# Constant products in the pauses of the opening, an earlier first shift block and another load order, in a one-core transformer block

## The chip, the cores and the metric

The kernel runs on one core of a Trainium2 chip. The time is that of one execution on the device in microseconds (us); lower is better. Three runs of the kernel before were timed, and one more execution was taken with the hardware profiler.

## The reference, cut to what matters

One layer of a diffusion backbone works on 256 latent tokens (x) and 256 context tokens (ctx), each with 1024 channels: a half-step feed-forward block, two token mixers side by side, a second half-step feed-forward block, a last norm. Everything is fp32. This change touches only the beginning:

```python
mod_x = (jax.nn.silu(c) @ w_ada[l] + b_ada[l])[:, None, :]
mod_c = (jax.nn.silu(c_ctx) @ w_ada[l] + b_ada[l])[None, None, :]
sh1x, sc1x, g1x, sh2x, sc2x, g2x, sh3x, sc3x, g3x = jnp.split(mod_x, N_MOD, axis=-1)
...
x = x + 0.5 * g1x * swiglu(modulate(rmsnorm(x, norm_ffn1[l]), sh1x, sc1x), w13_ffn1[l], w2_ffn1[l])
ctx = ctx + 0.5 * g1c * swiglu(modulate(rmsnorm(ctx, norm_ffn1[l]), sh1c, sc1c), w13_ffn1[l], w2_ffn1[l])
```

Here `modulate(h, shift, scale)` is `h * (1 + scale) + shift`, `rmsnorm` divides by the root of the mean square over the channels, and `swiglu` is `(silu(a) * b) @ w2` with `a, b = split(h @ w13)`. So before the first large product can start, two vectors (c and c_ctx) go through silu, are multiplied with blocks of w_ada, and the tokens are normed, scaled and shifted.

## The kernel before

Tokens lie as columns: 512 of them, 256 context and 256 latent, by eight blocks k of 128 channels (KT = 8). Every large product is made in fp32r as three products of split operands (`mm3`, lines 86 to 90): each operand is written as a high part (cast on ScalarE, ACT) and a low part (the difference, on VectorE, DVE), and lines 88 to 90 add low times high, high times low and high times high on TensorE (PE).

The *opening* (lines 97 to 408) has an order written out by hand for PE, ACT, DVE and SyncE (SP, which issues all loads). Behind it a planner, which simulates a timeline (line 30), orders the instructions of each engine. Loads that stand behind the opening in the program can be drawn by it to the front of SP's queue: the second load of the unit matrix (line 574) is issued as the second of all.

The opening goes like this.

1. SP loads the unit matrix, the two vectors c (`cr`, line 112), four tiles of x (`xs`, line 147, 512 KB each), and then for k = 0 and 1 (`first_loads`, line 150) the scale block of w_ada (`ada[KT + k]`), its shift block (`ada[k]`) and six column blocks of w13 (`w`, 384 KB). The table of small vectors (`sm`) comes between k = 0 and k = 1.
2. ACT takes silu of `cr` (162); PE turns it over (169, `ct`) and spreads each vector over all partitions (179, `cb`). A table load for the root follows on ACT (166).
3. ACT and DVE square the x blocks by turns (`sq`, 240 and 242), and PE sums them over the channels with a matrix `ones` of value 1/1024 (250, `st`): for each k four narrow products, eight instructions in fp32.
4. ACT takes the root (226), DVE the reciprocal (228), PE spreads the result over all partitions (262, `rs`: four fp32 products), ACT copies it (266, `rstd1`).
5. For each k: the *scale* column is a product and sum on DVE, one instruction per stream (191, `ada`), then the factor (200, `amul`) and the scaled tokens (364, `xr`). The *shift* column is made on PE: eight transposes of the shift block (277, `ada_turn`), two copies on ACT (280, `at`), sixteen narrow products (288, `ada_rows`), a copy (293, `row`), a small product (299) and the sum on DVE (300, `mod`, `ada_cols`). ACT adds the shift and writes the high part h1h (371), DVE the low part h1l (374). The weights of the block are split on ACT (351, `wh`) and DVE (352, `wl`).
6. PE adds the products of block k into six accumulators (`first_products`), two at a time; between them stand the steps of block k + 1 (lines 391 to 406).

On each engine the instructions of the opening run in this written order: what stands behind a waiting one waits too.

## Time and profile before

| what | us |
|---|---|
| median of three runs | 1014.06 |
| lowest, highest | 1011.98, 1014.34 |
| the profiled execution | 1015.47 |
| its span | 1013.7 |

The profiled execution lies 1.41 us above the median of the runs; its span is the time from its first to its last recorded work, and 1.77 us lie around it. All times in the trace count from the span's start. In lines of the timeline and of the views of waits stand the start, the duration, the engine, the line of the kernel, the operation, "out<-in", the shapes and how often (x4: four instructions drawn together); in brackets the idle time of that engine just before it and what ended it. PEld is the loading of a product's fixed operand, SPq the issue of a load by SP. A fp32 product of 128 columns appears as two instructions. In the chain of waits each line has the start, the duration and the work on the path that ended last. A line of the view by windows has the stretch, its length, the busy time (and instructions) of PE, PEld, DVE, ACT and POOL (GpSimd), the granted clock of PE, the busy share of the DMA engines and the GB/s that they moved.

### The profile page before, as it was taken

Reading aid. Unit: us, or ns where it says so; the run is one execution under the profiler, and the core shown is the slowest. Engines: PE = TensorE matmul, PEld = TensorE weight load, DVE = VectorE, ACT = ScalarE, POOL = GpSimd, SP = SyncE. Lnnn points to the kernel's source line nnn. Section 1 sums busy time; section 2 is a strip of 40 time slices with the busy share of each in tenths; the row PEclk is TensorE's granted clock in tenths of the full one; section 3 lists DMA queues with packets and bytes.
Section 4 is the critical chain, followed back from the end, with each engine's and each line's share of the span. In section 5 each row is a group of like instructions: output and inputs, shape, how many; then the busy total and the mean of one; then the engine's idle time right before and its main releaser. Section 6 shows DMA issues by size and latency. Waiting matters only on the chain.

```text
span 1013.7 us, 16779 instructions
## 1 busy us (share of the span) xinstructions
PE 984.4 (97%) x6792; PEld 907.9 (90%) x6792; DVE 663.9 (65%) x1084; ACT 469.4 (46%) x725; POOL 62.4 (6%) x39
## 2 busy tenths in 40 slices
PE   6999999999999998999999998999999989999996
PEld 4778888888888888999999997999999989999995
DVE  7879999998334335866575538865555766676543
ACT  4454322125222423756575456754444545555541
POOL 0000000000000013000000026000000300000011
PEclk9999999999999999999999999999999999999999
DMA  8647766994322233223133434456566446656651
GB/s 337 231 176 249 235 199 212 349 402 160 104 83 75 84 112 115 64 84 125 43 126 108 158 100 150 125 185 183 181 200 187 153 161 186 185 172 182 185 174 42
DMA packets 49238, 166.84 MB, mean 165 GB/s; under 512 B 5380, under 2 KB 7044, under 8 KB 49160
## 3 DMA queue, kind: packets, MB, share of 16 engines
q1 hardware_dynamic: 49160, 165.77, 50.8%
q8 instruction: 53, 0.87, 0.3%
q14 instruction: 25, 0.20, 0.1%
HBM read 164.70 MB, written 1.05 MB: 164 GB/s over the span
## 4 chain that ended last, share of the span: by engine, by line
PE 91%; DVE 4%; ACT 2%; DMA 1%; issue 1%; POOL 0%; DVEq 0%; SPq 0%; ACTq 0%; POOLq 0%
PE y L88 4%; PE y L89 4%; PE y L90 4%; PE pa L89 3%; PE pb L89 3%; PE pa L88 3%; PE pb L88 3%; PE pb L90 3%; PE pa L90 3%; PE ro L89 2%; PE ro L90 2%; PE ro L88 2%; PE fa L89 2%; PE z L90 2%; PE z L89 2%; PE z L88 2%
## 5 line engine op out<-in xcount | busy, mean ns | idle before, releaser
L79 DVE TENSOR_TENSOR wl<-wr,wh 128x1024 fp32r<-128x1024 f32 (+1 forms) x214 | 248.8, 1164 | 202.0 <-ACT wh L78 201.2
L78 ACT CAST wh<-wr 128x1024 fp32r<-128x1024 f32 (+1 forms) x226 | 227.0, 1006 | 273.2 <-PE y L90 79.2
L191 DVE CUSTOM_DVE_ANT_0 junk<-ada,cb,sm 128x1024 bf16<-128x1024 f32 x96 | 122.9, 1280 | 5.9 <-DMA ada<-in_ada 4.4
L89 PE MATMUL y<-gl,wh 128*128 128x512 f32 (+1 forms) x198 | 72.5, 366 | 0.0
L88 PE MATMUL y<-gh,wl 128*128 128x512 f32 (+1 forms) x198 | 72.4, 366 | 0.0
L90 PE MATMUL y<-gh,wh 128*128 128x512 f32 (+1 forms) x198 | 72.3, 365 | 0.0
L455 POOL TENSOR_TENSOR ssum<-ssum,sq 128x256 f32<-128x256 f32 (+1 forms) x18 | 24.6, 1367 | 727.3 <-ACT sq L454 714.2
L89 PE MATMUL pa<-h1l,wh 128*128 128x512 f32 x152 | 59.1, 389 | 0.0
L88 PE MATMUL pa<-h1h,wl 128*128 128x512 f32 x152 | 59.1, 389 | 0.0
L90 PE MATMUL pa<-h1h,wh 128*128 128x512 f32 x152 | 59.1, 389 | 0.0
L88 PE MATMUL pb<-h1h,wl 128*128 128x512 f32 x152 | 59.1, 389 | 0.0
L89 PE MATMUL pb<-h1l,wh 128*128 128x512 f32 x152 | 59.1, 389 | 0.0
L90 PE MATMUL pb<-h1h,wh 128*128 128x512 f32 x152 | 59.1, 389 | 0.0
L89 PE MATMUL fa<-hxl,wh 128*128 128x258 f32 x176 | 50.8, 289 | 0.0
L88 PE MATMUL fa<-hxh,wl 128*128 128x258 f32 x176 | 50.8, 289 | 0.0
L90 PE MATMUL fa<-hxh,wh 128*128 128x258 f32 x176 | 50.6, 287 | 0.0
L89 PE MATMUL fb<-hxl,wh 128*128 128x258 f32 x176 | 50.1, 284 | 0.0
L89 PE MATMUL z<-g2l,wh 128*128 128x256 f32 x176 | 50.0, 284 | 0.0
L88 PE MATMUL fb<-hxh,wl 128*128 128x258 f32 x176 | 50.0, 284 | 0.0
L90 PE MATMUL fb<-hxh,wh 128*128 128x258 f32 x176 | 49.9, 283 | 0.0
L88 PE MATMUL z<-g2h,wl 128*128 128x256 f32 x176 | 49.8, 283 | 0.0
L90 PE MATMUL z<-g2h,wh 128*128 128x256 f32 x176 | 49.8, 283 | 0.0
(310 smaller groups left out, 2908.3 us busy)
## 6 DMA issues: line engine op xcount, KB each, us to landing
ada<-in_ada SPq DMA_DIRECT2D x72, 512.0 KB, 5.1
wr<-in_w13b SPq DMA_DIRECT2D x44, 512.0 KB, 4.3
wr<-in_w13a SPq DMA_DIRECT2D x38, 512.0 KB, 4.3
wrv<-in_wv SPq DMA_DIRECT2D x16, 512.0 KB, 4.3
wr<-in_wg SPq DMA_DIRECT2D x16, 512.0 KB, 4.2
wr<-in_wgate SPq DMA_DIRECT2D x16, 512.0 KB, 4.3
wr<-in_pret SPq DMA_DIRECT2D x16, 512.0 KB, 3.8
wr<-in_w2b SPq DMA_DIRECT2D x16, 512.0 KB, 3.6
```

Source lines behind the costliest of these rows:

```text
L78: S.copy(hi[:, :n], raw[:, :n])
L79: (lo_engine or V).tensor_tensor(lo[:, :n], raw[:, :n], f32(hi[:, :n]), op=ALU.subtract)
L88: PE.matmul(o, w[1], a[0], start=start, stop=False)
L89: PE.matmul(o, w[0], a[1], start=False, stop=False)
L90: PE.matmul(o, w[0], a[0], start=False, stop=stop)
L191: V.tensor_tensor_reduce(junk, raw, cb[:, s, :], 1.0, sm[:, BIAS + n : BIAS + n + 1], ALU.mult, ALU.add, mod[:, s, n : n + 1],)
L455: G.tensor_tensor(ssum[0][:, cols], ssum[0][:, cols], sq[:, :w], op=ALU.add)
```

## The change

Five things, all in the opening but the last:

- *Order of loads.* The first x tile is loaded ahead of the vectors c. The table `sm` follows the x tiles directly. For each k the shift block is loaded ahead of the scale block.
- *Constant products* (`keep_warm`): `ones` times `ones`, 128 by 128 by 128 in fp32, into the bank that `ct` had or that `rs` will have; nobody reads the results. Six stand ahead of the transposes of `cr`, eleven among the sums of squares (1, 3, 4 and 3 ahead of those of k = 0, 2, 4 and 6), three behind them.
- *The first shift block* is transposed on PE (and copied on ACT) ahead of the spread of the reciprocal, instead of behind it, and its rows are made ahead of the first scale block's steps in the written order.
- *The split of the first weights* is cut in two: 256 columns ahead of h1h and h1l of block 0, 512 behind them, with the same work in all.
- *Two loads* (`dist` and the second `unit`), which the program has far behind the opening, are kept in the program's order.

```diff
+    xs = []
+
+    def load_x(q):
+        t = per.tile([P, 2, 512], F32, name=f"xs{q}")
+        nc.sync.dma_start(t, i["xs"][:, 2 * q : 2 * q + 2, :])
+        xs.extend([t[:, 0, :], t[:, 1, :]])
+
     unit_raw = stp.tile([P, P], F32, name="unit_raw")
     nc.sync.dma_start(unit_raw, i["unit"])
+    load_x(0)
     cr = wtile("wr", "cr")[:, :512]
...
-    for q in range(4):
-        t = per.tile([P, 2, 512], F32, name=f"xs{q}")
-        nc.sync.dma_start(t, i["xs"][:, 2 * q : 2 * q + 2, :])
-        xs += [t[:, 0, :], t[:, 1, :]]
+    for q in range(1, 4):
+        load_x(q)
+    nc.sync.dma_start(sm, i["smalls"])
 
     def first_loads(k):
-        for n in (KT + k, k):
+        for n in (k, KT + k):
...
     first_loads(0)
-    nc.sync.dma_start(sm, i["smalls"])
     first_loads(1)
...
     ps = bank("ct")
+
+    def keep_warm(o, n):
+
+        for _ in range(n):
+            PE.matmul(o, ones, ones, start=True, stop=True, skip_group_check=True)
+
+    idle = ps
+    keep_warm(idle[:, :P], 6)
     for c in range(4):
         PE.transpose(ps[:, c * P : (c + 1) * P], cr[:, c * P : (c + 1) * P], unit_raw)
...
+        keep_warm(idle[:, :P], (1, 0, 3, 0, 4, 0, 3, 0)[k])
         for q in range(4):
             PE.matmul(
                 ps_st[32 * q : 32 * q + 32, :P], ones[:, :32], sq[:, q * P : (q + 1) * P],
...
     r1 = rstd_of(ps_st[:, :P], P, "1q")
     ps_st = bank("rs1")
+    keep_warm(ps_st[:, :P], 3)
+    ada_turn(0)
     rstd1 = stp.tile([P, 512], F32, name="rstd1")
     for q in range(4):
         PE.matmul(
             ps_st[:, q * P : (q + 1) * P], pick[:, q * P : (q + 1) * P], r1, start=True, stop=True
         )
...
-    def first_split(k):
-        hi, lo = wtile("wh", f"wh0_{k}"), wtile("wl", f"wl0_{k}")
-        S.copy(hi[:, :n1], first_w[k][:, :n1])
-        V.tensor_tensor(lo[:, :n1], first_w[k][:, :n1], f32(hi[:, :n1]), op=ALU.subtract)
-        first_hl[k] = hi, lo
+    def first_split(k, c0=0, c1=n1):
+        if k not in first_hl:
+            first_hl[k] = wtile("wh", f"wh0_{k}"), wtile("wl", f"wl0_{k}")
+        c = slice(c0, c1)
+        split(first_hl[k][0][:, c], first_hl[k][1][:, c], first_w[k][:, c])
...
-    ada_turn(0)
+    ada_rows(0)
     first_scaled(0)
-    first_split(0)
-    ada_rows(0)
     ada_cols(0)
+    first_split(0, 0, T)
     first_shifted(0)
+    first_split(0, T, n1)
...
-    nc.sync.dma_start(dist, i["dist"])
+    tc.keep_in_program_order(nc.sync.dma_start(dist, i["dist"]))
...
-    nc.sync.dma_start(raw, i["unit"])
+    tc.keep_in_program_order(nc.sync.dma_start(raw, i["unit"]))
```

## The prediction, as put on record before the result

> **What bounds the kernel now.** I read the page first, then the chain of waits over the first 70 us, then the timeline of the same stretch engine by engine, and last the places where TensorE's clock changes.

> ```profile
> span 1013.7 us, 16779 instructions
> ...
> PE 984.4 (97%) x6792; PEld 907.9 (90%) x6792; DVE 663.9 (65%) x1084; ACT 469.4 (46%) x725; POOL 62.4 (6%) x39
> ```

> TensorE (PE) is busy for 97%, so what the change can win lies in the other 29 us and in the stretches where PE is busy but slow. The opening has most of both. Times and waits of its first part:

> ```profile
> 1.18 0.42 SPq L574 DMA_DIRECT2D unit<-in_unit  x1
> 1.65 0.67 SPq L112 DMA_DIRECT2D cr<-in_cc  x1
> 2.36 1.82 SPq L147 DMA_DIRECT2D xs<-in_xs  x4
> 3.75 0.63 ACT L162 ACTIVATE cr<-cr 128x512 f32<-128x512 f32 x1 [1.52 <-DMA cr<-in_cc]
> 4.39 1.28 ACT L166 ACT_TABLE_LOAD   x1
> 4.43 1.11 PE L169 MATMUL ct<-unit_raw,cr 128*128 128x128 f32 x4 [4.43 <-ACT cr L162]
> 5.69 0.29 ACT L166 ACTIVATE warm<-cr,eps 128x1 f32<-128x1 f32 x1
> 5.97 0.73 SPq L157 DMA_DIRECT2D sm<-in_smalls  x1
> 6.07 0.63 PE L179 MATMUL cb<-crl,one_r 1*128 1x512 f32 x4
> 6.11 0.63 ACT L242 ACTIVATE sq<-xs 128x512 f32<-128x512 f32 x1
> 11.41 1.08 PE L250 MATMUL st<-sq,ones 128*32 128x128 f32 x16 [0.17 <-ACT sq L242]
> 12.56 0.37 ACT L226 ACTIVATE sd1q<-st,eps 128x128 f32<-128x128 f32 x1 [1.20 <-PE st L250]
> 12.96 0.95 DVE L228 RECIPROCAL rstd1q<-sd1q 128x128 f32<-128x128 f32 x1
> 13.97 2.08 PE L262 MATMUL rs<-rstd1q,pick 128*128 128x128 f32 x8 [1.48 <-DVE rstd1q L228]
> 14.47 1.28 DVE L191 CUSTOM_DVE_ANT_0 junk<-ada,cb,sm 128x1024 bf16<-128x1024 f32 x1 [0.56 <-DMA sm<-in_smalls]
> ```

> The statistics (st) end at 12.49 (11.41 + 1.08), the reciprocal at 13.91, and DVE begins the first scale block at 14.47, held 0.56 by the small table sm. From there DVE's own queue sets the rhythm:

> ```profile
> 19.14 0.96 DVE L352 TENSOR_TENSOR wl<-w,wh 128x768 fp32r<-128x768 f32 x1 [0.79 <-ACT wh L351]
> ...
> 20.52 0.22 DVE L300 TENSOR_SCALAR mod<-tr,sm 128x2 f32<-128x2 f32 x1 [0.42 <-PE tr L299]
> ...
> 22.12 1.28 DVE L191 CUSTOM_DVE_ANT_0 junk<-ada,cb,sm 128x1024 bf16<-128x1024 f32 x1
> ...
> 27.02 0.96 DVE L352 TENSOR_TENSOR wl<-w,wh 128x768 fp32r<-128x768 f32 x1 [1.10 <-ACT wh L351]
> ...
> 29.49 1.28 DVE L191 CUSTOM_DVE_ANT_0 junk<-ada,cb,sm 128x1024 bf16<-128x1024 f32 x1
> ...
> 32.41 0.89 DVE L364 SCALAR_TENSOR_TENSOR xr<-xs,amul,rstd 128x256 f32<-128x256 f32 x2
> 33.21 0.95 DVE L352 TENSOR_TENSOR wl<-w,wh 128x768 fp32r<-128x768 f32 x1
> 34.07 0.22 DVE L300 TENSOR_SCALAR mod<-tr,sm 128x2 f32<-128x2 f32 x1
> 34.87 0.89 DVE L374 SCALAR_TENSOR_TENSOR h1l<-xr,mod,h1h 128x256 fp32r<-128x256 f32 x2 [0.58 <-ACT h1h L371]
> 35.67 1.28 DVE L191 CUSTOM_DVE_ANT_0 junk<-ada,cb,sm 128x1024 bf16<-128x1024 f32 x1
> ```

> A turn is one k of the opening, counted on DVE from one scale block to the next. Turn 0 takes 7.65 us (14.47 to 22.12), turn 1 7.37 (to 29.49), turn 2 6.18 (to 35.67). Turn 2 has one wait left, the 0.58 for ACT, and is what DVE can do. The excess of the first two turns is made of waits that end at PE: the 0.79 and 1.10 for wh stand behind copies in ACT's queue that wait for PE, the 0.42 is for PE itself. The chain has the reason and the end:

> ```profile
> 3.75 6.95 DMA xs<-in_xs
> ...
> 20.48 1.81 PE tr L277 x8
> ...
> 24.85 1.01 PE tr L288 x16
> ...
> 29.09 0.87 PE tr L277 x8
> ...
> 31.34 0.57 PE tr L288 x16
> ...
> 65.75 0.60 ACT h1h L371 x2
> ```

> The same eight transposes cost 1.81 and then 0.87, the same sixteen row products 1.01 and then 0.57: until about 25.8 PE runs at half speed. At 65.75 the chain leaves PE for h1h of the last block, which hangs on DVE's shift column. So DVE's queue ends the opening, and whatever brings DVE's turns forward brings the end forward.

> How the clock behaves shows later, where PE pauses:

> ```profile
> 813.50 0.70 PE L974 MATMUL st<-ssum,ones 128*128 128x256 f32 x2 [2.96 <-POOL ssum L455]
> ...
> 814.60 0.42 PE L89 MATMUL fa<-hxl,wh 128*128 128x258 f32 x1
> ...
> 817.83 0.29 PE L90 MATMUL fa<-hxh,wh 128*128 128x258 f32 x1
> ```

> After a pause of 2.96 the products go slow (0.42), and some 3.4 us of unbroken work later (about 814.4 to 817.8) fast again (0.29). I take 3.4 us of unbroken work as the least that raises the clock and twice that as the most, since such a stretch need not begin where the work does: in the opening, work without a break from 20.48 at the latest is fast only behind 25.86, more than 5 us later. A stretch that is not quite full did not do it:

> ```profile
> 18.99:22.40 3.41, 3.02 (x23) 2.52 (x16) 2.26 (x5) 1.78 (x6) 0.00 (x0) 1.00 1.02 404
> ```

> PE was busy for 3.02 of these 3.41 us, 89%, and stayed slow. The granted clock in this row reads 1.00 all the same; the half rate is read from the lengths of products alone.

> **The change part by part.** *Loads.* The first x tile takes the issue slot of unit at 1.18 instead of 2.36. For landings:

> ```profile
> DMA to landing us min/median/max: 3.7/5.5/7.0
> ```

> That is the line for the x tiles: the first lands at 6.06 (2.36 + 3.7), now 1.18 earlier, 4.88. cc stands behind it in SP's queue. Its landing is between 3.75 (not delayed) and 4.88 (behind the whole tile). I take 4.7, near the upper end, because sm, 64 KB, was issued at 5.97 behind larger loads and was waited for until 14.47, while unit, as large, with nothing before it, took:

> ```profile
> unit<-in_unit SPq DMA_DIRECT2D x1, 64.0 KB, 1.9
> ```

> So silu of cr ends at 5.33, 0.95 later than now, and sq on ACT can start at 7.06 (4.7 + 2.36, with the table load between); ACT and DVE have six operations of at most 0.7 each from there, so all squares are there by about 11.2. The fourth x tile landed at 10.7 (in the chain, 3.75 + 6.95), so a 512 KB tile takes 1.55 ((10.7 - 6.06)/3). sm now follows the x tiles and costs nothing: the 0.56 goes. The first shift block lands at about 11.3 (4.88 + 4 x 1.55 + 0.2), the scale block, now second, at 12.8, both before their use below; were the shift block later than PE's turn to it, the reciprocal's spread would queue behind it. The same exchange for the other blocks is hidden: they are loaded two turns ahead.

> *Constant products, 20 of 128x128x128 in fp32.* The nearest row is rs: four such products, eight instructions, 13.97 to the transposes behind them, at 0.23 to 0.26 each, so 0.47 a product at the slow clock; fast, two instructions like a transpose (0.87/8), 0.22. The six before the transposes of cr need only ones, which DVE sets among its first instructions (about 1.6, an estimate); they take 2.8, to 4.4, and end before cr is there: free. The eleven among the statistics and the three behind them stand in PE's queue ahead of real work. The first of them also waits for DVE's copies out of ct's bank, which are done before the cb products. The three behind the statistics have the 1.4 us of root and reciprocal as cover.

> *Statistics.* PE takes up the cr transposes at 5.38; slow, they and cb need 2.27 (4.43 to 6.70), to 7.65. Then eleven products (5.17 slow, 2.42 fast) and four pairs of statistics (4 x 1.08 slow; 4 x 0.57 fast, by the row products of the same shape): 9.49 slow, 4.70 fast. PE has no pause from 5.38 on, so the clock rises between 8.8 (5.38 + 3.4) and 12.2 (5.38 + 6.8). Rising at 8.8, the statistics end at 7.65 + 1.15 + 8.34 x 0.495 = 12.93; at 12.2, at 14.65; in the middle, 10.5, at 13.79. I take the middle: 1.3 later than now. This is the price of the fill.

> *From there to DVE's first turn.* Root and reciprocal take 1.42 as now and DVE starts 0.05 behind them: statistics' end + 1.47 instead of + 1.98. In the cover PE does three products and the eight transposes (0.66 + 0.87), then the spread (0.87 at the fast clock), so rstd is copied by + 3.5, before DVE needs it at + 4.4 (2.92 behind its start, 29.49 to 32.41). Rows and columns of the shift follow on PE and are ready before DVE has scaled.

> *Turn 0* is then 2.92, 0.80 (32.41 to 33.21), 0.80 (column to h1l, 34.07 to 34.87), 0.80 (h1l) and two thirds of the split's 0.86, 0.58: 5.90; the first third lies in the wait for ACT. That saves 1.75. *Turn 1* has PE at the fast clock with its transposes already done and becomes like turn 2: 1.19 saved. If PE should pause before the first products and fall back to the slow clock, there is slack: six slow products (0.43 each) and the rows (1.01) end 3.6 after h1h, and copy and cast behind them 1.1 later, while DVE needs wh some 4.9 after h1h.

> *Two loads in program order* (dist, unit): small, and first needed hundreds of us later; nothing, either way.

> Sum: 1.75 + 1.19 + 0.51 + 12.49 - 13.79 = 2.15 us, or 15.94 minus the statistics' end. Next late is DVE with ACT, 6.18 a turn. The profiled execution would go from 1015.47 (span 1013.7 and 1.77 around it) to 1013.3. It is 1.4 above the median of the three runs, so against the median I say 1014.06 - 2.15 = 1011.9.

> **Rivals.** *The clock is up before the statistics.* If the six products and what follows count as one stretch, PE is fast from 5.4 on. Then the statistics wait for sq (7.69) and need ten products and four pairs from there (4.48): 12.2, a gain of 3.7. With 8.8 giving 3.0, this case is 3.4: 1010.7. For it: with cc at 3.75 PE would have no gap from 1.6 on. Against it: the gap of 0.9 from 4.4 to 5.33, if cc is late, and the row above in which 89% was not enough.

> *Transposes do not raise the clock.* If they count as pause, the stretch starts at 6.4, behind the four of cr, the clock rises between 9.8 and 13.2, the statistics end at 13.4 to 15.2, gain 0.8 to 2.5: 1012.4 in the middle. For it: the 3.02 of that row are mostly transposes (1.81 from 20.48 on alone). [...]

> *The fill never pays.* If the constant products do not raise the clock, all 9.49 are done slow: statistics' end 17.14, DVE's first turn at 18.6, 4.1 late, the spread behind slow products and transposes (1.41 + 1.81 + 1.87 + 0.65 for the copies = 5.7 where DVE needs it at 4.4, so turn 0 takes some 7.3 instead of 5.9), turn 1 as slow as now: 4.1 + 7.3 - 7.65 = 3.8 slower, 1017.9. It decides from a rise after 14.8, where the sum is zero. Against it: the rows at 814 to 818 show 3.4 us to be enough.

> *Given back behind the opening.* The order of the rest comes from a planner that simulates time, and there the loads are full:

> ```profile
> 70.00:75.00 5.00, 5.00 (x24) 4.14 (x23) 1.26 (x2) 0.70 (x2) 0.00 (x0) 1.00 1.00 388
> ```

> 388 GB/s at a DMA share of 1.00: if loads or a new order of the rest take the 2.15, the time stays at 1014.1, give or take 2. Against it: PE is busy through all of this stretch.

> **How the numbers follow.** Forecast 0.45 (own range 1010.8 to 1012.9); clock up early 0.25; transposes 0.10; given back 0.12; never pays 0.08. The range, 1009.2 to 1014.8, takes in the first three with some 1.5 us for the spread of medians (the three runs span 2.4) and most of the fourth. 0.3% is 3.04 us, about what a measurement can tell from no change. Faster by more: 0.8 of the early case, a quarter of the forecast, some of the rest: 0.36. Slower by more: most of "never pays" and a third of "given back": 0.11. Within: 0.53.

> **What would show it.** Right: silu of cr near 4.7; PE busy without pause from 5.4; the change of product length between 8.8 and 12.2; statistics ending near 13.8; DVE's first scale block 1.5 behind that with no wait for sm; turns of 5.9, then 6.2; h1h of the last block some 2 us earlier. Wrong: statistics ending before 12.5 or behind 15.9, a wait for wh in turn 1, or a gain at 66 us that is not there at the end.

## The result, and the profile after

| | median of the runs | lowest to highest | profiled execution, span |
|---|---|---|---|
| before, beside the changed kernel | 1012.88 us (14) | 1011.98 to 1014.74 | 1015.47, 1013.7 |
| after | 1015.32 us (14) | 1014.06 to 1016.46 | 1014.82, 1013.0 |

The ratio is 1.002, 95% interval [1.0012, 1.0028]: the changed kernel is slower by 0.2%, 2.44 us between the medians, where 2.15 less was forecast. Note that the two profiled executions stand the other way round: before's is above every one of its 14 runs, after's is below its median. In all the series of this document together two executions ran at a granted clock of 0.66 and took 1376.14 and 1378.85 us; the ratios leave them out.

The page of the changed kernel:

```profile
span 1013.0 us, 16861 instructions
...
PE 987.7 (97%) x6832; PEld 910.9 (90%) x6832; DVE 664.6 (66%) x1085; ACT 468.2 (46%) x726; POOL 62.3 (6%) x39
```

Forty instructions (twenty products) more on PE and 3.3 us more of busy time. The opening from the timeline (start, length, what; in brackets the idle time before it and what ended it):

```profile
1.60 2.93 PE L178 MATMUL ct<-ones 128*128 128x128 f32 x12 [1.60 <-DVE ones L126]
4.78 0.63 ACT L168 ACTIVATE cr<-cr 128x512 f32<-128x512 f32 x1 [2.55 <-DMA cr<-in_cc]
5.46 1.12 PE L183 MATMUL ct<-unit_raw,cr 128*128 128x128 f32 x4 [0.93 <-ACT cr L168]
7.66 0.80 PE L178 MATMUL ct<-ones 128*128 128x128 f32 x2
8.39 1.08 PE L265 MATMUL st<-sq,ones 128*32 128x128 f32 x16
9.40 1.65 PE L178 MATMUL ct<-ones 128*128 128x128 f32 x6
10.98 1.08 PE L265 MATMUL st<-sq,ones 128*32 128x128 f32 x16
11.35 0.63 ACT L256 ACTIVATE sq<-xs 128x512 f32<-128x512 f32 x1 [0.94 <-DMA xs<-in_xs]
11.99 1.71 PE L178 MATMUL ct<-ones 128*128 128x128 f32 x8
13.63 0.64 PE L265 MATMUL st<-sq,ones 128*32 128x128 f32 x16
14.21 0.94 PE L178 MATMUL ct<-ones 128*128 128x128 f32 x6
15.07 0.65 PE L265 MATMUL st<-sq,ones 128*32 128x128 f32 x16
15.79 0.37 ACT L240 ACTIVATE sd1q<-st,eps 128x128 f32<-128x128 f32 x1 [3.81 <-PE st L265]
16.18 0.95 DVE L242 RECIPROCAL rstd1q<-sd1q 128x128 f32<-128x128 f32 x1 [2.67 <-ACT sd1q L240]
17.05 1.18 DVE L205 CUSTOM_DVE_ANT_0 junk<-ada,cb,sm 128x1024 bf16<-128x1024 f32 x1
23.06 1.28 DVE L205 CUSTOM_DVE_ANT_0 junk<-ada,cb,sm 128x1024 bf16<-128x1024 f32 x1
26.77 0.95 DVE L84 TENSOR_TENSOR wl<-w,wh 128x768 fp32r<-128x768 f32 x1
29.23 1.28 DVE L205 CUSTOM_DVE_ANT_0 junk<-ada,cb,sm 128x1024 bf16<-128x1024 f32 x1
65.17 0.90 ACT L388 ACTIVATE h1h<-xr,mod 128x256 fp32r<-128x256 f32 x2
```

Read the statistics first. The first x16 row takes 1.08, the last 0.65; the clock rises inside the x8 row at 11.99, near 13.1. The statistics end at 15.72 (15.07 + 0.65), 3.23 later than before. The squares are not what they wait for: ACT begins the last of them at 11.35. ACT waits 3.81 for PE, then DVE 2.67 for ACT: this is the wait that took the place of the one for sm. Behind it everything is as planned: turn 0 takes 6.01 (17.05 to 23.06), turn 1 6.17, the wait for wh ahead of wl in turn 1 is gone. So the two turns give back what the statistics cost, and h1h of the last block starts at 65.17 instead of 65.44, on ACT's timeline of the kernel before:

```profile
65.44 0.91 ACT L371 ACTIVATE h1h<-xr,mod 128x256 fp32r<-128x256 f32 x2
```

That is a gain of 0.27 between these two executions.

### The profile page after: what moved, and what is told of

The parts are those of the page before. It is cut to its first block, busy times and chain, and to the rows that moved or that the text cites. A ratio compares the mean times of both kernels' runs of the same rounds, so it can differ in the third digit from the quotient of the medians.

```text
span 1013.0 us, 16861 instructions
## 1 busy us (share of the span) xinstructions
PE 987.7 (97%) x6832; PEld 910.9 (90%) x6832; DVE 664.6 (66%) x1085; ACT 468.2 (46%) x726; POOL 62.3 (6%) x39
## 4 chain that ended last, share of the span: by engine, by line
PE 90%; DVE 5%; ACT 2%; issue 1%; DMA 1%; POOL 0%; DVEq 0%; ACTq 0%; POOLq 0%
PE y L88 4%; PE y L90 4%; PE y L89 4%; PE pa L90 3%; PE pb L90 3%; PE pa L88 3%; PE pb L88 3%; PE pa L89 3%; PE pb L89 3%; PE ro L89 2%; PE ro L88 2%; PE ro L90 2%; PE z L89 2%; PE z L90 2%; PE z L88 2%; PE fa L89 2%
## 5 line engine op out<-in xcount | busy, mean ns | idle before, releaser
L89 PE MATMUL y<-gl,wh 128*128 128x512 f32 (+1 forms) x198 | 72.7, 367 | 0.0
L90 PE MATMUL y<-gh,wh 128*128 128x512 f32 (+1 forms) x198 | 72.5, 366 | 0.0
L89 PE MATMUL pa<-h1l,wh 128*128 128x512 f32 x152 | 59.2, 390 | 0.0
L90 PE MATMUL pa<-h1h,wh 128*128 128x512 f32 x152 | 59.2, 390 | 0.0
L89 PE MATMUL pb<-h1l,wh 128*128 128x512 f32 x152 | 59.2, 390 | 0.0
L90 PE MATMUL pb<-h1h,wh 128*128 128x512 f32 x152 | 59.2, 390 | 0.0
L90 PE MATMUL fa<-hxh,wh 128*128 128x258 f32 x176 | 50.6, 287 | 0.0
L89 PE MATMUL fa<-hxl,wh 128*128 128x258 f32 x176 | 50.5, 287 | 0.0
L89 PE MATMUL z<-g2l,wh 128*128 128x256 f32 x176 | 50.1, 285 | 0.0
L89 PE MATMUL fb<-hxl,wh 128*128 128x258 f32 x176 | 50.0, 284 | 0.0
L90 PE MATMUL fb<-hxh,wh 128*128 128x258 f32 x176 | 50.0, 284 | 0.0
L90 PE MATMUL z<-g2h,wh 128*128 128x256 f32 x176 | 49.9, 284 | 0.0
```

What stands on the lines that cost most here:

```text
L89: PE.matmul(o, w[0], a[1], start=False, stop=False)
L90: PE.matmul(o, w[0], a[0], start=False, stop=stop)
```

## The experiments

The theory after this reading: the eleven products among the statistics stand ahead of real work in PE's queue, and since cc lands 1.0 later with the new order of the loads, PE pauses 0.93 behind the six products and does more than half of the fill at half speed. The rivals: the new order of the loads costs by itself (x tiles late); the new order of the turn, or of dist and unit, costs by itself; and the forecast's base, one execution of the kernel before, was an uncommon one, so that there was less to gain. All ratios are to the kernel before, run on the same chip beside each. Its median was 1013.42 (35 runs) beside no fill, the loads alone, dist and unit alone and the turn's order alone; 1013.64 (27) beside twice the fill, no products, the old loads and before once more; 1013.37 (31) beside the last four. A ratio is not the quotient of the two medians and can differ from it by some 0.1%: for eight products first it is 0.9991, where the medians give 1.0001.

**No fill among the statistics.** The changed kernel without line

```
-        keep_warm(idle[:, :P], (1, 0, 3, 0, 4, 0, 3, 0)[k])
```

> The changed kernel without the eleven constant products among the sums of squares; six ahead of the transposes of cr and three behind the statistics stay. Theory 1 (the products stand in TensorE's queue ahead of the statistics and cost more than the reordered turns bring): the statistics end near 12.7 instead of 15.7 us (last square 12.04, then 0.54 to 0.6), DVE starts turn 0 near 14.2 instead of 17.05, turn 0 is some 1.4 longer because spread and transposes are slow again, turn 2 starts near 27.5 instead of 29.2: some 1.7 us faster than the changed kernel, 1.000 to 1.001 of the kernel before. Theory 2 (the load order is what costs, through the later c vectors and last x tile) and theory 3 (two loads in program order, or the planner's order of the rest, cost behind the opening): no change, 1.002.

Measured: 1012.24 us, 0.9989 [0.9979, 0.9998]. From its timeline on PE:

```profile
5.60 0.65 PE L183 MATMUL ct<-unit_raw,cr 128*128 128x128 f32 x4 [1.08 <-ACT cr L168]
...
7.73 0.64 PE L264 MATMUL st<-sq,ones 128*32 128x128 f32 x16 [0.43 <-ACT sq L256]
9.40 1.08 PE L264 MATMUL st<-sq,ones 128*32 128x128 f32 x16 [1.03 <-ACT sq L256]
...
12.00 1.08 PE L264 MATMUL st<-sq,ones 128*32 128x128 f32 x16 [0.21 <-ACT sq L256]
```

The clock is up right behind the six products here (0.65 for the transposes that take 1.12 in the changed kernel). Each pair of statistics now waits for its squares, and although the clock falls again (0.64, then 1.08) the last one ends at 13.08, 2.64 earlier than in the changed kernel. Taking eleven products away turns +0.2% into -0.1%, somewhat better than the 1.000 to 1.001 that was expected.

**Twice the fill.**

```
-        keep_warm(idle[:, :P], (1, 0, 3, 0, 4, 0, 3, 0)[k])
+        keep_warm(idle[:, :P], (2, 0, 6, 0, 8, 0, 6, 0)[k])
```

> The changed kernel with twice the constant products among the sums of squares (22 instead of 11). Theory 1 (they stand in TensorE's queue ahead of the statistics, and the clock rises near 13.4 us either way): eleven more at 0.22 (fast) to 0.47 us (slow) delay the statistics by 2.4 to 3.5 us, and the whole run by as much against the changed kernel: ratio to before 1.0045 to 1.0055. Rival (the loss is not the queue, but an accident of order or loads): 1.002 as the changed kernel.

Measured: 1016.67 us, 1.0032 [1.0019, 1.0044]. The transposes of cr, the first pair and the last, from PE's timeline:

```profile
5.84 0.66 PE L183 MATMUL ct<-unit_raw,cr 128*128 128x128 f32 x4 [1.31 <-ACT cr L168]
...
8.26 1.08 PE L265 MATMUL st<-sq,ones 128*32 128x128 f32 x16
...
16.42 0.64 PE L265 MATMUL st<-sq,ones 128*32 128x128 f32 x16
```

Eleven more products end the statistics 1.34 later, at 17.06, less than expected: in this execution most of them are done at the full clock, which is up at 5.84, down by 8.26 and rises again near 11, where the changed kernel's rises near 13. The reciprocal on DVE waits 4.33 for ACT, and ACT for PE. So the fill is on the path here too; the interval of the ratio overlaps that of the changed kernel, so the addition is read from the trace, not from the times.

**The order of the loads alone**, with dist and unit in program order; and **dist and unit alone**. Of the first:

```
     unit_raw = stp.tile([P, P], F32, name="unit_raw")
     nc.sync.dma_start(unit_raw, i["unit"])
+    load_x(0)
...
+    for q in range(1, 4):
+        load_x(q)
+    nc.sync.dma_start(sm, i["smalls"])
...
-        for n in (KT + k, k):
+        for n in (k, KT + k):
```

> The kernel before with the new load order alone (first x tile ahead of the c vectors, the small table behind the x tiles, shift blocks ahead of scale blocks, dist and unit in program order). Theory 1: silu of cr 1.0 later, statistics end at 12.6 instead of 12.5, the wait of 0.56 for the small table gone: 0.4 us faster than before, ratio 0.9995 to 1.000. Theory 2: the whole loss is here, ratio 1.002. Theory 3: the same 1.002, and then order_only has it too.

> The kernel before with only dist and the second unit load kept in program order. Theories 1 and 2: no change, ratio 1.000 (the unit load leaves 64 KB at the front, 0.2 us at most). Theory 3: ratio 1.002, and the stages behind the opening are longer by some 2 us.

Measured: 1013.25 us, 1.0002 [0.9991, 1.0014], for the loads; 1014.28 us, 1.0003 [0.9993, 1.0012], for dist and unit. Neither shows a cost or a gain. What the loads' new order does to cc is there without any product: silu of cr starts at 4.89 on ACT's timeline,

```profile
4.89 0.63 ACT L168 ACTIVATE cr<-cr 128x512 f32<-128x512 f32 x1 [2.66 <-DMA cr<-in_cc]
```

against 3.75 before. In this kernel the delay costs little, because the statistics wait for squares anyway: they end at 12.80 instead of 12.49.

**The turn's new order alone** (the shift block first on PE, rows earlier, the split in two; old loads, no products).

```
     ps_st = bank("rs1")
+    ada_turn(0)
     rstd1 = stp.tile([P, 512], F32, name="rstd1")
...
-    ada_turn(0)
+    ada_rows(0)
     first_scaled(0)
-    first_split(0)
-    ada_rows(0)
     ada_cols(0)
+    first_split(0, 0, T)
     first_shifted(0)
+    first_split(0, T, n1)
```

> The kernel before with the first shift block turned over ahead of the spread, its rows ahead of the first scale block, the split in two, dist and unit in program order; no constant products, old load order otherwise. Theory 1: turn 0 goes from 7.65 to some 6.7 us and turn 1 from 7.37 to some 7: 1.0 to 1.5 us faster than before, ratio 0.9985 to 0.999. Theory 2: 1 to 3 us faster, ratio 0.997 to 0.999. Theory 3: slower by 0.001 or more.

Measured: 1012.48 us, 0.9995 [0.9985, 1.0006]. In its profile turn 0 takes 6.84 and turn 1 6.18, and h1h of the last block starts at 62.86, 2.58 earlier than in before's profile; of that the medians show 0.9, and the interval of the ratio reaches above 1.

**The changed kernel without any of the twenty products.**

```
-    keep_warm(idle[:, :P], 6)
...
-        keep_warm(idle[:, :P], (1, 0, 3, 0, 4, 0, 3, 0)[k])
...
-    keep_warm(ps_st[:, :P], 3)
```

> The changed kernel without any of the twenty constant products. Theory 1 with useful products at the ends (six ahead of the c vectors, three behind the statistics raise the clock where TensorE waits anyway): 0.5 to 1.5 us slower than no_fill, ratio to before 0.9993 to 1.0003. Rival (constant products bring nothing anywhere): as no_fill, 0.9989 or less.

Measured: 1012.13 us, 0.9986 [0.9977, 0.9995], the same as without the eleven alone. The six and the three are free, but bring nothing that these intervals can show: turns of 6.00 and 6.17 come without them.

**All twenty products with the order of the loads of before.**

```
-    load_x(0)
...
-        for n in (k, KT + k):
+        for n in (KT + k, k):
...
     first_loads(0)
+    nc.sync.dma_start(sm, i["smalls"])
```

> The changed kernel, all twenty constant products in it, with the load order of before (but dist and unit in program order). Theory 1: the c vectors come 1.0 us earlier, TensorE's queue starts 1.0 earlier, the fill has more pauses to lie in and may rise with the first six in one stretch; the statistics end 1 to 2 us earlier than 15.7: ratio to before 0.9985 to 1.001. Rival (the fill costs 3 us wherever it stands): 1.002.

Measured: 1012.59 us, 0.9984 [0.9975, 0.9993]. This is the run that shows the products as such to be without cost. PE's timeline:

```profile
1.60 2.93 PE L172 MATMUL ct<-ones 128*128 128x128 f32 x12 [1.60 <-DVE ones L118]
4.32 1.06 PE L177 MATMUL ct<-unit_raw,cr 128*128 128x128 f32 x4
...
6.13 0.49 PE L172 MATMUL ct<-ones 128*128 128x128 f32 x2
...
11.15 0.64 PE L259 MATMUL st<-sq,ones 128*32 128x128 f32 x16
...
17.57 1.09 PE L272 MATMUL tr<-unit_raw,ada 128*128 128x128 f32 x8 [1.41 <-DMA ada<-in_ada]
```

cr is there when the six products end, so no bracket stands behind the transposes. The clock is up from the first product of the fill (0.49 for one, where the changed kernel has 0.80), and the statistics end at 11.79 with the whole fill among them. The old loads cost elsewhere: 0.65 for sm, and 1.41 in turn 1 for the shift block, which comes second in this order.

**The kernel before once more.** No edit.

> The kernel before, unchanged, as a kernel of its own. Its ratio to before shows what five rounds can tell: 1.000 within 0.001. Theory 4 (the profiled execution of before from which the sums were made had a late rise of the clock, 25.8 us, and the time of before differs from run to run with that rise): the opening of this execution need not have the rise at 25.8, and where it is earlier, turns 0 and 1 are shorter. Rival (the rise stands where it is in every execution): again turns of 7.65 and 7.37 us.

Measured: 1013.71 us, 1.0001 [0.9992, 1.0011]. Its profile is of another execution. PE's timeline, then DVE's:

```profile
19.90 1.07 PE L277 MATMUL tr<-unit_raw,ada 128*128 128x128 f32 x8
```

```profile
21.67 1.28 DVE L191 CUSTOM_DVE_ANT_0 junk<-ada,cb,sm 128x1024 bf16<-128x1024 f32 x1
...
25.39 0.95 DVE L352 TENSOR_TENSOR wl<-w,wh 128x768 fp32r<-128x768 f32 x1
27.85 1.28 DVE L191 CUSTOM_DVE_ANT_0 junk<-ada,cb,sm 128x1024 bf16<-128x1024 f32 x1
```

Here the second block's transposes take 1.07 (1.95 in before's profile): the clock is up near 19 (the last section shows where) and not at 25.8. Turn 1 takes 6.18 and has no wait for wh: the 1.19 that the forecast saves there isn't there to be saved. h1h of the last block starts at 63.78, 1.66 earlier than in the execution the forecast was made from. And yet this profiled execution took 1014.79, only 0.68 less than the other one and 1.08 above the median of its own series.

**cc ahead of the first x tile.** The changed kernel with all its products and

```
-    load_x(0)
     cr = wtile("wr", "cr")[:, :512]
     V.memset(cr, 0.0)
     nc.sync.dma_start(cr.rearrange("(q r) n -> q r n", r=32)[:, 0, :], i["cc"])
+    load_x(0)
```

> The changed kernel with all twenty products, only the first x tile's load put behind that of cc. Theory (the fill costs because cc is late: the six products end before cr is there, PE pauses, and the eleven products are then done at the slow rate): cr is there by about 4, the six products run into its transposes without a pause, the clock rises by about 6, the statistics end at 12.0 to 12.8 instead of 15.7, and the time is 0.998 to 0.999 of the kernel before, as with the old loads. Rival (the fill in the queue costs whenever the new load order slows the x tiles): the statistics end behind 14.5, ratio 1.001 to 1.003. A third way (the rise has its own phase and is chance): statistics between, ratio about 1.000.

Measured: 1011.99 us, 0.9982 [0.9974, 0.9991]. One small load moved by one place takes the whole cost away. But the clock rises later than expected. PE's timeline:

```profile
1.60 2.93 PE L178 MATMUL ct<-ones 128*128 128x128 f32 x12 [1.60 <-DVE ones L126]
4.32 1.06 PE L183 MATMUL ct<-unit_raw,cr 128*128 128x128 f32 x4
5.31 0.80 PE L193 MATMUL cb<-crh,one_r 1*128 1x512 f32 x4
...
9.78 0.80 PE L265 MATMUL st<-sq,ones 128*32 128x128 f32 x16
...
13.04 0.65 PE L265 MATMUL st<-sq,ones 128*32 128x128 f32 x16
```

From 1.60 on PE has no pause at all, and yet runs at half speed until about 10.1, inside the row at 9.78. The statistics end at 13.69, not at 12.0 to 12.8. That is 2.03 earlier than in the changed kernel: 1.20 of it is the fill's earlier start (6.46 for 7.66), the rest the clock's earlier rise. So "no pause, hence a fast clock" is too simple.

**Eight products instead of six ahead of cr.**

```
-    keep_warm(idle[:, :P], 6)
+    keep_warm(idle[:, :P], 8)
```

> The changed kernel with its late cc, and eight products instead of six ahead of the transposes of cr, so that they last to 1.6 + 8 x 0.48 = 5.4, when cr is there. Theory (the pause of 0.9 is what keeps the clock down): no pause, the clock up by about 6, statistics' end at 12.2 to 13.0, held by the last x tile, ratio 0.998 to 0.9995. Rival (the pause does not matter, PE in the transposes and narrow products counts as idle and the rise comes near 13 as in the changed kernel): statistics' end 15.5 to 16.2, ratio 1.002 to 1.003.

Measured: 1013.51 us, 0.9991 [0.9981, 1.0002]; the interval lies below that of the changed kernel. PE's timeline:

```profile
1.60 3.78 PE L178 MATMUL ct<-ones 128*128 128x128 f32 x16 [1.60 <-DVE ones L126]
5.67 1.11 PE L183 MATMUL ct<-unit_raw,cr 128*128 128x128 f32 x4 [0.28 <-ACT cr L168]
6.71 0.50 PE L193 MATMUL cb<-crh,one_r 1*128 1x512 f32 x4
...
12.46 0.65 PE L265 MATMUL st<-sq,ones 128*32 128x128 f32 x16
```

cc is as late as in the changed kernel, the pause is 0.28, and the clock is up at 6.7 (0.50 for what took 0.80). The statistics end at 13.11. This profiled execution, 1011.98, is the third lowest of eleven and 1.53 below their median, so it need not stand for the others.

**cc ahead of the first x tile, and no products**: the loads of the run above, and the three lines taken out as further up.

> None of the twenty products, and the first x tile's load behind that of cc: what is left is the order of the loads and the turn's new order. Theory (the products are worth nothing, the new order of the turn and sm early are the gain): ratio 0.998 to 0.999, statistics' end about 12.5, first scale block about 13.9, no wait for sm. Rival (the products, where they run on without a pause, are worth a rise of the clock of their own): cc_first is faster than this one by 0.1% or more.

Measured: 1010.95 us, 0.9975 [0.9965, 0.9985], the lowest time of the study. The last pair of statistics and the transposes behind it, on PE's timeline:

```profile
10.71 1.08 PE L263 MATMUL st<-sq,ones 128*32 128x128 f32 x16 [0.21 <-ACT sq L255]
11.72 1.97 PE L276 MATMUL tr<-unit_raw,ada 128*128 128x128 f32 x8
```

All statistics are done slow, and end at 11.79: PE waits for the squares of each of the four pairs, 0.59, 0.16, 0.19 and 0.21. The shift block's transposes lie in the shadow of the reciprocal at half speed (1.97), and it doesn't matter. The rival, that products which run on without a pause are worth something, finds no support: cc_first with its products has 0.9982, this one 0.9975, the intervals overlapping.

**The changed kernel once more.** No edit.

> The changed kernel once more. If its cost is in the opening and does not hang on one execution's clock: statistics' end again between 15 and 17, the first scale block at 16.5 to 18, ratio 1.001 to 1.003. If the phase of the clock decides, as it did for the kernel before (rise at 25.8 and at 19): statistics' end anywhere between 12.5 and 17, and a ratio that may be below 1.001.

Measured: 1015.07 us, 1.0015 [1.0006, 1.0023]. Statistics' end 15.78, first scale block 17.12, the clock up near 13: the cost is not one execution's chance.

## Why the prediction was wrong

The forecast's sum was "15.94 minus the statistics' end". Against h1h of the last block (65.44 in before's profile) it holds in every kernel that has the three edits and no further wait; the statistics' end is the last row of st, start and length added:

| kernel | statistics' end | 15.94 - end | h1h earlier by | span less by |
|---|---|---|---|---|
| after | 15.72 | 0.22 | 0.27 | 0.7 |
| after once more | 15.78 | 0.16 | 0.21 | 0.3 |
| twice the fill | 17.06 | -1.12 | -1.07 | -1.2 |
| no fill | 13.08 | 2.86 | 2.90 | 3.8 |
| no products | 12.94 | 3.00 | 3.05 | 4.5 |
| eight first | 13.11 | 2.83 | 2.86 | 3.5 |
| cc first, no products | 11.79 | 4.15 | 4.21 | 4.6 |

Two versions have a further wait. In cc_first (13.69) the sum gives 2.25 and h1h is 1.92 earlier: turn 1 takes 6.56 and has a wait of 0.30 for wh ahead of wl. With the old loads (11.79) it gives 4.15, and h1h is 2.91 earlier, for the waits named there. So the mechanism was right from the statistics on, and in these profiled executions h1h's gain stays to the end: of the rival "given back behind the opening" they show nothing. Point by point:

- *Loads.* silu of cr was forecast at 4.7 and starts at 4.78; the wait for sm is gone; the last squares start at 11.35, where the forecast had all squares done by 11.2. (One reading behind the 4.7 was wrong without harm: unit had a load ahead of it, unit_raw, issued at 0.74.)
- *From the statistics to the scale block.* 1.47 forecast, 1.33 measured (15.72 to 17.05).
- *Turns.* 5.90 and 6.18 forecast, 6.01 and 6.17 measured.
- *The statistics: this step failed.* "PE has no pause from 5.38 on, so the clock rises between 8.8 (5.38 + 3.4) and 12.2 (5.38 + 6.8)", and in the middle the statistics end at 13.79. The clock rose near 13.1 and they ended at 15.72, 1.93 later. Of that, 0.86 is the choice of the middle: by the forecast's own 12.2 they end at 14.65. The products were mis-sized too: three take 1.58 slow (9.40 to 10.98) and 0.86 fast (14.21 to 15.07), 0.53 and 0.29 apiece against the 0.47 and 0.22 taken from rows of the spread; with these lengths and a rise at 12.2, the rows above give 15.3, 0.67 more. The remaining 0.4 is a clock that rose behind the bound. The 3.4 us in that bound were misread as well: in before's profile the work behind the late pause runs from 813.50, a product at 814.15 still takes 0.29, and they are slow from 814.4 on. So the 3.4 to the rise are the distance from a fall of the clock to its rise, not the length of work that raised it.
- *Why it rose so late.* The forecast counted one-row products and the narrow statistics as work that raises the clock like any other. The row of cc_first is the plainest against that: no pause from 1.60, and half speed to 10.1. The other part is where the steps of the last section lie. In two versions with a late cc, no fill and twice the fill, the clock was up right behind the six products (the transposes of cr take 0.65 and 0.66, against 1.12 in the changed kernel) and down again by 9.40 and 8.26. Counted back in steps of 3.4 from the next rise, near 15.1 in no fill (inside eight transposes that take 1.37, between the 1.97 and the 1.04 of other versions) and near 11.2 in twice the fill, the steps lie near 1.5 and 4.9 and near 1.0 and 4.4, so that nearly all of the six products (1.60 to 4.53) lies between two of them. In the changed kernel, counted back from 13.1, one lies at 2.9, which parts them. So where an execution's steps lie may have a share in its statistics' end, and these single profiles do not separate it from the edit. The rival "Transposes do not raise the clock" gave a rise at 9.8 to 13.2, nearer to what came, but not for its reason: the last section shows a stretch, 1.9 of its 3.4 us transposes, at whose end it rose.
- *The base: this step failed as well.* "It is 1.4 above the median of the three runs, so against the median I say 1014.06 - 2.15". The savings were worked out in one execution, which lies 2.59 above the median of before's fourteen runs beside the changed kernel (the median of the three runs, 1014.06, lies 1.18 above it), and the forecast took the whole sum off the median nevertheless. What lifted that execution stays open. Its late rise of the clock, at 25.8, is at most a part of it: in before_again the clock rose near 19 and 1.66 of the savings were not there, but that profile is above its median as well. Nor is the late rise an uncommon one: with dist and unit alone, and with the loads alone, the clock rises near 25.7 and 26.1.

As a sum: 2.15 forecast less 1.93 is 0.22, and h1h is 0.27 earlier. The profiled executions differ by 0.65 (1015.47 to 1014.82); what is gained behind h1h is not explained here. Between the medians it is +2.44, because before's median lies 2.59 below its profiled execution and after's 0.50 above (-0.65 + 2.59 + 0.50). So the statistics took away most of the forecast gain, and the base turned what was left into a loss. Between versions that share the new turn the base plays no part: from the changed kernel to no fill h1h is 2.63 earlier, the profiled execution 3.17 shorter and the median 3.08 lower.

What the parts are worth: the order of loads 1.0002 and the turn's order 0.9995, neither of them clear of 1, both without products 0.9986; the eleven products add about 0.3% to this when cc is late (1.0020 and 1.0015, against 0.9989 without them), and nothing that these intervals can show when cc is early (0.9982 and 0.9984). Shown is that the cost needs both the fill and the late cc: each alone is without cost. The two are not enough by themselves: with eight products first cc is as late and the fill as long, and the cost is gone (0.9991). That it is the clock's late rise that makes the difference fits the profiles, but the rise was not set by itself.

## What to carry to other kernels

Work put into an engine's pauses stands ahead of the real work in that engine's queue: it is free only up to the moment the real work is ready, so check the latest input against the fill at its slow price, and a small load that gates the engine goes ahead of a large one in its queue (here one line, 0.4% between 1.0020 and 0.9982). Take a saving from several executions, not from one, when a state such as the clock's differs between them: the two profiles of the kernel before lie 1.66 apart at h1h, and a profiled time above the median is a reason to take a second profile. And a fill that should raise the clock has to be tested against the same kernel without it: here the best version without products (0.9975) is not slower than the same with them (0.9982).

## What the runs showed of the hardware

**The distances between the clock's changes differ by steps of 3.4 us.** In before's profile the clock rises near 25.86, falls near 814.4 and rises again near 817.8: 3.4 from the fall to the rise, 791.9 between the rises. The later changes, behind a pause of 2.95 to 2.98 us that every version has somewhere between 805 and 816, can be read to 0.1 us. The product in which it rises, on PE's timeline of the changed kernel, of cc_first and of eight_first:

```profile
818.57 0.36 PE L88 MATMUL fb<-hxh,wl 128*128 128x258 f32 x1
```

```profile
815.49 0.38 PE L89 MATMUL fb<-hxl,wh 128*128 128x258 f32 x1
```

```profile
815.45 0.38 PE L89 MATMUL fb<-hxl,wh 128*128 128x258 f32 x1
```

**What lies in the 3.4 us ahead of a step.** The steps here are counted back from the rise in the opening, 10.1 in cc_first. There the stretch from 3.3 to 6.7 is full: 1.3 us of products of 128x128x128 (3.3 to 4.3, and from 6.46), 1.0 of transposes, 1.15 of one-row products, no pause. The clock did not rise. The next one, 6.7 to 10.1, holds 2.0 of such products (0.45 and 1.58) and 1.4 of statistics, and it rose. In eight_first the stretch from 3.3 to 6.7 holds 2.1 of them, 1.0 of transposes and a pause of 0.28, and it rose. The statistics, 32 columns wide, are seen nearly by themselves in the kernel without products, on PE's timeline:

```profile
8.70 1.08 PE L263 MATMUL st<-sq,ones 128*32 128x128 f32 x16
10.00 2.94 PE L263 MATMUL st<-sq,ones 128*32 128x128 f32 x48 [0.22 <-ACT sq L255]
12.87 1.97 PE L276 MATMUL tr<-unit_raw,ada 128*128 128x128 f32 x8
```

Its clock rises near 15.1 (inside the spread at 14.63, which takes 1.31, where before's slow one takes 2.08 and the changed kernel's 1.06), so a step lies at 11.7; the 3.4 us before it hold at least 2.7 us of statistics and 0.4 of one-row products, and the clock did not rise: the transposes at 12.87 are slow. Transposes with little else are seen in before_again:

```profile
15.73 1.91 PE L277 MATMUL tr<-unit_raw,ada 128*128 128x128 f32 x8
18.32 0.94 PE L288 MATMUL tr<-at,ct 128*32 128x128 f32 x16 [0.68 <-ACT at L280]
```

Here the stretch from 15.6 to 19.0 holds some 1.9 of transposes, 0.7 of row products and 0.1 of the spread, with 0.68 of pause, and the clock rose (0.94 for the row products that take 1.08 slow). So a rise followed 3.4 us that are mostly transposes. Whether they do less than other work of the same length is not settled, since almost the same stretch, 15.7 to 19.1, did not raise the clock in before's own profile, where the second block's transposes, at 20.34, still take 1.95:

```profile
15.84 1.92 PE L277 MATMUL tr<-unit_raw,ada 128*128 128x128 f32 x8
18.43 1.08 PE L288 MATMUL tr<-at,ct 128*32 128x128 f32 x16 [0.67 <-ACT at L280]
```

In these stretches narrow work, of one row or of 32 columns, did less to raise the clock than wide work of the same length. Some 2.3 us of wide work and transposes, with 1.15 of one-row products, did not raise it (cc_first); 2.0 with 0.7 of 32 columns did once and did not the other time. How much is enough was not measured by itself.

What sets where the steps lie stays open. Counted back in steps of 3.4 from the rise in the opening, the first of them lies between 0.5 (cc first without products) and 3.3 (cc_first) in the fourteen executions, while the two kernels that were profiled twice come out within 0.2 of themselves; so a part of the differences of 0.1% between versions may come from it, and none of them is explained here. Nor is it settled which of before's two rises, at 25.8 and near 19, is the more frequent.

**A small load behind a large one.** With one 512 KB x tile issued ahead of it on the same queue, cc is there later. It is issued at 1.65 both in before's profile and in the changed kernel's, and silu of cr starts at 3.75 in the one and at 4.78, behind the x tile, in the other. In all seven profiles with that order silu starts at 4.78 to 5.82 (the latest without products), and PE, which waits for it, takes up the transposes of cr at 5.46 to 6.50. In the five profiles where neither an x tile is ahead of cc nor a product ahead of these transposes, they start at 4.03 to 4.43.
